# Splitting half of the convolution mixers' weight blocks on GpSimd instead of VectorE

## The chip, the cores and the metric
The kernel runs on one core of one Trainium2 chip. The metric is device time in microseconds (us) of one launch; the median of three runs before the change is 2242.76 us (2242.38 to 2246.66).

The core's engines are named as the profile names them: PE (TensorE matmuls), PEld (TensorE weight loads, which overlap PE), DVE (VectorE), ACT (ScalarE), POOL (GpSimd) and SP (SyncE, which here only issues DMAs). Each engine takes its own instructions strictly in order and waits at an instruction until what it needs has been signalled by the others.

## The reference
One inference step of a four-layer decoder trunk (1024 channels) for 256 prompt tokens and 8 x 4 sample tokens, 288 columns in all. Every layer is a token mixer and a squared-ReLU MLP with residuals; layers 0 and 3 use retention, layer 1 Mamba-2 SSD, layer 2 gated DeltaNet.

```python
for i in range(DEPTH):                       # DEPTH = 4
    h = _rms(x, norm_mix[i])
    out = (_retention, _ssd, _gdn)[i % 3](h, ...)
    x = x + out
    x = x + jnp.square(jax.nn.relu(_rms(x, norm_mlp[i]) @ w_up)) @ w_down

def _ssd(h, ...):                            # _gdn has the same frame
    z, xbc, dt = split(h @ w_in)             # 1024 x 6176 weights
    xbc, new_buf = _causal_conv(xbc, conv_buf, conv_w)   # 4 taps
    xbc = silu(xbc + conv_b)
    y, s_new = _decay_scan(c_out, b_in, xs * dt, log_a, s0)
    return _rms(y * silu(z)) * norm_w @ w_out            # 2048 x 1024 weights
```

The two mixers with a causal convolution in front of their scan, SSD and gated DeltaNet, are the "convolution mixers" of this text. All inputs and outputs are fp32.

## The kernel before
Activations lie transposed: 128 channels on the partitions, 288 tokens along the free dimension. Every product with a weight matrix goes through one routine, `dense` (lines 188 to 232). To keep fp32 precision with the fast fp32r matmul, it splits each operand into a high and a low part and adds three products: high x high, low activations x high weights, high activations x low weights (lines 227, 228, 229).

The weights pass through three steps. SP loads a block `raw` of 1 MB (two buffers). The block is cut along its columns into tiles, and each tile along the contraction into two halves of 128 x 512 elements: the loop over `kh` at line 207, whose first half has `kh` = 0. For each half ACT writes the high part, `wh` (line 212, a cast to fp32r), and then DVE the low part, `wl` = raw - wh (line 215):

```python
self.last_cast = nc.scalar.copy(wh, src)
nc.vector.tensor_tensor(out=wl, in0=src, in1=wh, op=ALU.subtract)
```

`wh` and `wl` have four buffers each, so two tiles are held. A tile of two halves feeds 24 matmuls of 288 columns. Both splitting instructions are issued at high priority (`HP`), so the scheduler, which writes the fixed order of every engine's queue ahead of time from priorities and its own cost estimates, sets them early.

`units` (lines 510 to 535) runs a mixer in four units. Of unit m it weaves the chain of small steps that the scan needs (`step(m)`: the finish of unit m-1, then `chain(m)`) with dense work that fills PE meanwhile: the gate projection, the output projection of an earlier unit, and the input projection of unit m+1. At the entry, before any weaving, `proj(0)` runs alone; at the end `out(3)` runs alone. The names of the chain that come up below:

- entry of SSD and gated DeltaNet: `ms` (line 333, DVE) and `rs_y` (line 268, a power on POOL) make the norm's factor, which PE broadcasts; then the step sizes go through a softplus on DVE (lines 883 to 894) to `la` (line 996, SSD) or `g` (line 1315), on which the first cumulative sums on PE wait.
- convolution: `U` gets the past columns by a copy on POOL (line 808), `cacc` adds the taps on DVE (line 832), `tl` keeps the last columns (line 818 at first, on DVE).
- SSD unit: `xw`, `xws`, `bm`, `cm` are products on POOL (lines 1062, 1078, 1114, 1112), `Et` the decay matrices (line 1167).
- gated DeltaNet unit (`prep`): `L` (line 1484, DVE, eight instructions), `Et` (line 1493, POOL), `kd` (line 1542, POOL), `Ls` (line 1498 on, DVE), `sm` (lines 1535 to 1537, DVE), `lm` (line 1565, POOL), `T` (line 1568, DVE) and then `ps_Y` on PE.

`gates_tok` calls `dense` with weights that are already loaded (`pre`), for the 32 columns of the step sizes.

Of the kernel before, what the change touches and what calls it, by code (L numbers as in the profile page):

```python
# [12 lines left out]
ALU = mybir.AluOpType  # L13
# [110 lines left out]
def run(gen):  # L124
    for _ in gen:
        pass


class K:
    def __init__(self, ctx, tc, I, O, C, layers):  # L130
        self.tc, self.nc, self.I, self.O, self.C = tc, tc.nc, I, O, C
        self.layers = layers
        self.hold, self.started = [], False
        self.ahead = 0
        nc = self.nc
        E = ctx.enter_context
        self.const = E(tc.tile_pool(name="const", bufs=1))
        self.xp = E(tc.tile_pool(name="xp", bufs=1))
        self.raw = E(tc.tile_pool(name="raw", bufs=2))
        self.wsp = E(tc.tile_pool(name="wsp", bufs=4))  # L140
        self.actp = E(tc.tile_pool(name="actp", bufs=1))
        self.tmp = E(tc.tile_pool(name="tmp", bufs=3))
        self.psd = E(tc.tile_pool(name="psd", bufs=3, space=PSUM))
        self.psm = E(tc.tile_pool(name="psm", bufs=5, space=PSUM))

        def cload(name, shape=None, src=None):
            a = I[name] if src is None else src
            t = self.const.tile(list(a.shape) if shape is None else shape, F32, name="c_" + name)
            nc.sync.dma_start(t, a)
            return t  # L150

        self.ones = self.const.tile([128, 128], F32, name="ones")
        nc.vector.memset(self.ones, 1.0)
        self.mhalf = self.const.tile([128, 1], F32, name="mhalf")
        nc.vector.memset(self.mhalf, -0.5)
        self.vec = self.const.tile([128, 128], F32, name="vec")
        with tc.high_priority(1000):
            self.ident = cload("ident")
# [29 lines left out]
    def dense(self, xh, xl, w, evac, pre=None):  # L188
        nc, tc = self.nc, self.tc
        n, kt = w.shape[1], len(xh)  # L190
        cw = 2048 // kt
        sw = 1024 // kt
        for c0 in range(0, n, cw):
            cn = min(cw, n - c0)
            if pre is None:
                raw = self.raw.tile([128, kt, cn], F32, name="raw", tag="raw")
                with self.tc.high_priority(HP):
                    step = cn if self.started or c0 else sw
                    for s0 in range(0, cn, step):
                        self.last_load = nc.sync.dma_start(raw[:, :, s0:s0 + step],  # L200
                                          w[:, c0 + s0:c0 + s0 + step].rearrange("(k p) n -> p k n", p=128))
            else:
                raw = pre
            for s0 in range(0, cn, sw):
                sn = min(sw, cn - s0)
                hs, ls = [], []
                for kh in range(0, kt, kt // 2):
                    wh = self.wsp.tile([128, kt // 2, sn], F32R, name="wh", tag="wh")
                    wl = self.wsp.tile([128, kt // 2, sn], F32R, name="wl", tag="wl")
                    src = raw[:, kh:kh + kt // 2, s0:s0 + sn]  # L210
                    with self.tc.high_priority(HP):
                        self.last_cast = nc.scalar.copy(wh, src)  # L212
                        first = self.hold.pop(0) if self.hold else None
                        with tc.issue_after(first.ins) if first else nullcontext():
                            nc.vector.tensor_tensor(out=wl, in0=src, in1=wh, op=ALU.subtract)  # L215
                    hs += [wh[:, k] for k in range(kt // 2)]
                    ls += [wl[:, k] for k in range(kt // 2)]
                for o in range(0, sn, 128):
                    os = slice(o, min(o + 128, sn))
                    self.ahead -= 1  # L220
                    if 0 <= self.ahead < 2:
                        ps = self.ps("psd", "s")[:, 0:T]
                    else:
                        ps = self.psd.tile([128, T], F32, name="psd", tag="d")
                    po = ps[:os.stop - o]
                    for k in range(kt):
                        nc.tensor.matmul(po, lhsT=hs[k][:, os], rhs=xh[k], start=(k == 0), stop=False)  # L227
                        nc.tensor.matmul(po, lhsT=hs[k][:, os], rhs=xl[k], start=False, stop=False)  # L228
                        self.last_mm = nc.tensor.matmul(po, lhsT=ls[k][:, os], rhs=xh[k], start=False,  # L229
                                                        stop=(k == kt - 1))  # L230
                    evac((c0 + s0 + o) // 128, ps)
                    yield kt * 3 * 0.124
# [274 lines left out]

        yield from self.dense(act[0], act[1], w[m * 512:(m + 1) * 512, :], ev)

    def units(self, proj, chain, gate, fin, w, i, side=None):  # L510
        acts = {}

        def finish(m):
            acts[m] = self.act_quarter(m)
            yield from fin(m, *acts[m])

        def out(n):
            yield from self.w_out(w, n, acts.pop(n), i)

        def step(m):  # L520
            if m:
                yield from finish(m - 1)
            yield from chain(m)

        self.ahead = 5
        run(proj(0))
        for m in range(4):
            fill = [gate(m)]
            fill += [out(0)] if m == 1 else [out(1)] if m == 3 else []
            rest = [proj(m + 1)] if m < 3 else []  # L530
            if side:
                rest = [self.both(side(m), rest[0])] if rest else [side(m)]
            self.weave(step(m), *fill, *rest)
        self.weave(finish(3), out(2))
        run(out(3))


# [400 lines left out]
    def ssd(self, ctx, j, i):  # L938
        nc, tc, I, O, C = self.nc, self.tc, self.I, self.O, self.C
# [3 lines left out]
        w = I["ssd_w_in"][j]  # L943
# [92 lines left out]
        units = {}  # L1036
# [203 lines left out]
                                           op0=ALU.mult, op1=ALU.mult)  # L1240
                    self.split(o, ah[a], al[a])

        self.units(proj, scan, gate, fin, I["ssd_w_out"][j], i)

# [2 lines left out]
    def gdn(self, ctx, j, i):  # L1249
        nc, tc, I, O, C = self.nc, self.tc, self.I, self.O, self.C  # L1250
# [3 lines left out]
        w = I["gdn_w_in"][j]  # L1254
# [101 lines left out]
        units = {}  # L1356
# [400 lines left out]
            yield from prep(m)  # L1757
            yield from loop(m)

        self.units(proj, scan, gate, fin, I["gdn_w_out"][j], i, sample)  # L1760
        self.later = lambda pool: self.gdn_states(pool, j)

    def gdn_states(self, pool, j):
# [83 lines left out]
```

## Time and profile before
| | |
|---|---|
| median of 3 runs | 2242.76 us |
| profiled execution, its own time | 2250.74 us |
| its span, first to last instruction | 2248.6 us |
| mean granted TensorE clock | 0.98 of full speed |
| PE, PEld busy | 97 %, 89 % of the span |
| DVE, ACT, POOL busy | 69 %, 55 %, 26 % |
| SSD mixer | about 536 to 890 us of the span |
| gated DeltaNet mixer | about 1088 to 1480 us |

The profiled execution is one run of its own, 8.0 us above the median of the others. A matmul's busy time is longer than its share of PE's pace, because matmuls are pipelined: each of 288 columns is shown as 0.29 us, but the next starts 0.13 us later. So PE's idle time, the granted clock and what PE waited for say more than its busy share. In the two convolution mixers DVE and POOL work on the chains beside the weights; in the MLPs they do little else than the weights, the evictions and the residual.

### The profile page before, as it was taken

How to read it: one execution, taken by the hardware profiler on the slowest of the kernel's cores; microseconds unless marked ns; L12 is line 12 of the kernel's file. 1: busy time of each engine (PE TensorE's matmuls, PEld its weight loads, DVE VectorE, ACT ScalarE, POOL GpSimd, SP SyncE). 2: the span in 40 equal slices, each digit the busy share in tenths (PEclk: the TensorE clock that was granted, in tenths of full speed). 3: DMA queues.
4: the chain of work that ended last, by engine and by line, in shares of the span. 5: the costliest groups of instructions: out<-in, count | busy, mean ns of one | idle time of the engine just before them, and what ended most of it. 6: DMA issues, size and time to landing. Idle time of an engine off the chain costs nothing. (4 is left out here: it accounts for less than half of the span.)

```text
span 2248.6 us, 43174 instructions
## 1 busy us (share of the span) xinstructions
PE 2172.1 (97%) x16348; PEld 1996.7 (89%) x16348; DVE 1555.2 (69%) x3195; ACT 1242.9 (55%) x2823; POOL 586.0 (26%) x622
## 2 busy tenths in 40 slices
PE   9999999999999999999899999999999999999998
PEld 7878899998889889999888888889899779889998
DVE  6777775557898887555786786577766677776554
ACT  4444455545687766554466676476644444445454
POOL 2100113333322322333332232134333001103333
PEclk9999999999899999999989999899999999999999
DMA  7776765545446544554443442277765666764553
GB/s 208 255 254 206 248 195 160 169 151 161 128 145 192 171 143 139 172 169 151 148 127 106 121 140 93 90 207 236 226 187 188 228 230 218 237 222 158 163 167 115
DMA packets 404219, 394.96 MB, mean 176 GB/s; under 512 B 13003, under 2 KB 353716, under 8 KB 403916
## 3 DMA queue, kind: packets, MB, share of 16 engines
q1 hardware_dynamic: 403852, 391.96, 55.0%
q8 instruction: 128, 2.10, 0.4%
q14 instruction: 79, 0.65, 0.1%
q10 hardware_dynamic: 96, 0.20, 0.0%
q0 software_dynamic: 64, 0.07, 0.0%
HBM read 333.49 MB, written 58.69 MB: 174 GB/s over the span
## 5 line engine op out<-in xcount | busy, mean ns | idle before, releaser
L212 ACT CAST wh<-raw 128x512 fp32r<-128x512 f32 x1024 | 627.8, 620 | 675.4 <-PE psd L228 629.7
L215 DVE TENSOR_TENSOR wl<-raw,wh 128x512 fp32r<-128x512 f32 x1024 | 743.3, 733 | 309.0 <-ACT wh L212 290.5
L227 PE MATMUL psd<-xh,wh 128*128 128x288 f32 x2576 | 776.4, 302 | 6.5 <-ACT xh L302 4.6
L228 PE MATMUL psd<-xl,wh 128*128 128x288 f32 x2576 | 773.4, 300 | 4.4 <-DVE xl L303 3.2
L229 PE MATMUL psd<-xh,wl 128*128 128x288 f32 x2576 | 770.3, 299 | 3.8 <-DVE wl L215 3.8
L227 PEld LDWEIGHTS psd<-xh,wh 128*128 128x128 f32 x2576 | 487.7, 190 | 27.5 <-issue 11.1
L228 PEld LDWEIGHTS psd<-xl,wh 128*128 128x128 f32 x2576 | 491.6, 191 | 18.2 <-issue 7.5
L229 PEld LDWEIGHTS psd<-xh,wl 128*128 128x128 f32 x2576 | 490.7, 191 | 11.6 <-DVE wl L215 6.7
L227 PE MATMUL psd<-ah,wh 128*128 128x288 f32 x1536 | 463.4, 302 | 5.0 <-DVE x L447 2.8
L229 PE MATMUL psd<-ah,wl 128*128 128x288 f32 x1536 | 459.8, 299 | 6.8 <-DVE wl L215 6.7
L228 PE MATMUL psd<-al,wh 128*128 128x288 f32 x1536 | 460.8, 300 | 1.6 <-issue 1.1
L227 PEld LDWEIGHTS psd<-ah,wh 128*128 128x128 f32 x1536 | 292.6, 191 | 15.3 <-ACT wh L212 5.3
L229 PEld LDWEIGHTS psd<-ah,wl 128*128 128x128 f32 x1536 | 293.9, 191 | 10.2 <-DVE wl L215 9.1
L228 PEld LDWEIGHTS psd<-al,wh 128*128 128x128 f32 x1536 | 293.3, 191 | 10.0 <-issue 7.8
L487 POOL TENSOR_TENSOR x<-x,dn 128x288 f32<-128x288 f32 x120 | 148.7, 1239 | 239.4 <-DVE dn L485 239.4
L468 POOL TENSOR_TENSOR a<-v 128x288 f32<-128x288 f32 x128 | 109.6, 857 | 270.7 <-ACT v L467 269.7
L731 DVE SCALAR_TENSOR_TENSOR S<-S,ps_up 128x512 f32<-128x512 f32 x128 | 83.4, 685 | 53.5 <-PE ps_up L730 50.8
L832 DVE SCALAR_TENSOR_TENSOR cacc<-U,cw,cacc 128x312 f32<-128x312 f32 x192 | 105.3, 554 | 13.8 <-ACT cacc L827 11.8
L470 DVE TENSOR_TENSOR al<-a,ah 128x288 fp32r<-128x288 f32 x128 | 59.9, 468 | 68.7 <-POOL a L468 67.9
L268 POOL TENSOR_TENSOR rs_y<-ms,mhalf 128x3 f32<-128x3 f32 (+3 forms) x37 | 36.2, 981 | 231.2 <-DVE ms L747 170.7
L808 POOL COPY U<-cb 128x24 f32<-128x24 f32 x64 | 34.4, 543 | 208.0 <-DVE cacc L832 140.4
L485 DVE TENSOR_TENSOR dn<-psd,rb 128x288 f32<-128x288 f32 x128 | 58.2, 455 | 40.4 <-PE psd L229 40.4
(512 smaller groups left out, 2618.5 us busy)
## 6 DMA issues: line engine op xcount, KB each, us to landing
raw<-mlp_w_up SPq DMA_DIRECT2D x64, 1024.0 KB
raw<-mlp_w_down SPq DMA_DIRECT2D x64, 1024.0 KB
raw<-ret_w_in SPq DMA_DIRECT2D x32, 1024.0 KB
S<-state_ret SPq DMA_DIRECT2D x64, 512.0 KB
s_ret<-S SPq DMA_DIRECT2D x64, 512.0 KB
raw<-ssd_w_in SPq DMA_DIRECT2D x24, 1024.0 KB
raw<-gdn_w_in SPq DMA_DIRECT2D x24, 1024.0 KB
raw<-ret_w_in SPq DMA_DIRECT2D x32, 512.0 KB
```

What stands on the lines that cost most here:

```text
L212: self.last_cast = nc.scalar.copy(wh, src)
L215: nc.vector.tensor_tensor(out=wl, in0=src, in1=wh, op=ALU.subtract)
L227: nc.tensor.matmul(po, lhsT=hs[k][:, os], rhs=xh[k], start=(k == 0), stop=False)
L228: nc.tensor.matmul(po, lhsT=hs[k][:, os], rhs=xl[k], start=False, stop=False)
L229: self.last_mm = nc.tensor.matmul(po, lhsT=ls[k][:, os], rhs=xh[k], start=False, stop=(k == kt - 1))
L268: self.nc.gpsimd.tensor_tensor(out=y[rows], in0=ms[rows], in1=self.mhalf[rows].broadcast_to([rows.stop - rows.start, n]), op=ALU.pow)
L468: nc.gpsimd.tensor_tensor(out=a, in0=v, in1=v, op=ALU.mult)
L470: nc.vector.tensor_tensor(out=al[o], in0=a, in1=ah[o], op=ALU.subtract)
L485: nc.vector.tensor_tensor(out=t, in0=ps, in1=rb2, op=ALU.mult)
L487: e.tensor_tensor(out=self.x[o], in0=self.x[o], in1=t, op=ALU.add)
L731: nc.vector.scalar_tensor_tensor(out=S[:, b, z], in0=S[:, b, z], scalar=C["g4"][h], in1=up, op0=ALU.mult, op1=ALU.add)
L832: nc.vector.scalar_tensor_tensor(out=acc[:, 0:n], in0=u, scalar=wk, in1=acc[:, 0:n], op0=ALU.mult, op1=ALU.add)
```

## The change
`dense` picks the engine of the low part: while `share` is set, the second half of every tile (`kh` not 0, and not the preloaded gate weights) is subtracted by GpSimd; the first half, and everything outside, stays on VectorE. `units` sets `share` for its whole run except `out(3)`; only `ssd` and `gdn` ask for it.

```diff
+        self.share = False
...
-                            nc.vector.tensor_tensor(out=wl, in0=src, in1=wh, op=ALU.subtract)
+                            e = nc.gpsimd if self.share and kh and pre is None else nc.vector
+                            e.tensor_tensor(out=wl, in0=src, in1=wh, op=ALU.subtract)
...
-    def units(self, proj, chain, gate, fin, w, i, side=None):
+    def units(self, proj, chain, gate, fin, w, i, side=None, share=False):
...
         self.ahead = 5
+        self.share = share
         run(proj(0))
...
         self.weave(finish(3), out(2))
+        self.share = False
         run(out(3))
...
-        self.units(proj, scan, gate, fin, I["ssd_w_out"][j], i)
+        self.units(proj, scan, gate, fin, I["ssd_w_out"][j], i, share=True)
...
-        self.units(proj, scan, gate, fin, I["gdn_w_out"][j], i, sample)
+        self.units(proj, scan, gate, fin, I["gdn_w_out"][j], i, sample, share=True)
```

In the queues, 120 of the 1044 `wl` instructions go from DVE to POOL, 60 in each mixer; the orders of the other engines change a little inside these two mixers, and nowhere else. Lines of the changed kernel are 2 to 4 higher.

POOL's queue in the `prep` of the last gated DeltaNet unit, before (`rs_y` and `eq` end the norms of queries and keys; `T` and `Sd` come after `lm`):

```order
L268 TENSOR_TENSOR rs_y<-ssq,mhalf 128x10
L1444 TENSOR_SCALAR eq<-ssq 128x4
L1445 TENSOR_SCALAR eq<-ssq 128x1
L1493 TENSOR_TENSOR Et<-Et,gm 128x256 x4
L1542 TENSOR_TENSOR kd<-ktok,ge 128x512 x2
L1565 TENSOR_TENSOR lm<-sm,c_gdn_lms 128x128
L1582 TENSOR_TENSOR at_18436<-sm,c_gdn_b_11523 128x128
L1565 TENSOR_TENSOR lm<-sm,c_gdn_lms 128x128
L1533 COPY T_13996<-Tm 32x8x32 x2
```

and the same place in the changed kernel:

```order
L217 TENSOR_TENSOR wl<-raw,wh 128x512 x2
L270 TENSOR_TENSOR rs_y<-ssq,mhalf 128x10
L1448 TENSOR_SCALAR eq<-ssq 128x4
L1449 TENSOR_SCALAR eq<-ssq 128x1
L1497 TENSOR_TENSOR Et<-Et,gm 128x256 x3
L217 TENSOR_TENSOR wl<-raw,wh 128x512
L1497 TENSOR_TENSOR Et<-Et,gm 128x256
L1546 TENSOR_TENSOR kd<-ktok,ge 128x512 x2
L217 TENSOR_TENSOR wl<-raw,wh 128x512
L1569 TENSOR_TENSOR lm<-sm,c_gdn_lms 128x128
L1586 TENSOR_TENSOR at_18436<-sm,c_gdn_b_11523 128x128
L1569 TENSOR_TENSOR lm<-sm,c_gdn_lms 128x128
```

Two `wl` now stand ahead of `rs_y`, one between the third and fourth `Et` and one between `kd` and `lm`.

DVE's queue at that place, from the `L` on, before:

```order
L1484 SCALAR_TENSOR_TENSOR L<-Et,be_18148,gm 128x128 x8
L215 TENSOR_TENSOR wl<-raw,wh 128x512 x3
L1498 STREAM_TRANSPOSE Ls<-Lc 128x512
L1535 TENSOR_TENSOR sm<-ps_gram_18102,c_gdn_m_11529 128x32
L1499 TENSOR_SCALAR Ls<-Ls,c_gdn_h_11533 128x256
L1536 SCALAR_TENSOR_TENSOR sm<-ps_gram_18102,sc_18154,c_gdn_m_11529 128x32
L1500 SCALAR_TENSOR_TENSOR Ls<-Ls,c_gdn_h_11533 128x256
L1537 TENSOR_TENSOR sm<-sm,e_17945 128x64
```

and in the changed kernel:

```order
L1488 SCALAR_TENSOR_TENSOR L<-Et,be_18148,gm 128x128 x8
L217 TENSOR_TENSOR wl<-raw,wh 128x512
L552 SCALAR_TENSOR_TENSOR sg<-th,psd 128x288
L1539 TENSOR_TENSOR sm<-ps_gram_18102,c_gdn_m_11529 128x32
L1540 SCALAR_TENSOR_TENSOR sm<-ps_gram_18102,sc_18154,c_gdn_m_11529 128x32
L1502 STREAM_TRANSPOSE Ls<-Lc 128x512
L217 TENSOR_TENSOR wl<-raw,wh 128x512
L1503 TENSOR_SCALAR Ls<-Ls,c_gdn_h_11533 128x256
L1541 TENSOR_TENSOR sm<-sm,e_17945 128x64
L1504 SCALAR_TENSOR_TENSOR Ls<-Ls,c_gdn_h_11533 128x256
```

Behind the eight `L` there stood three `wl`, now one, and `sm` moves up before `Ls`.

DVE's queue at the entry of SSD, before (`ms` starts the norm's factor):

```order
L303 SCALAR_TENSOR_TENSOR xl_6500<-x_93,vec,xh_6499 128x288
L215 TENSOR_TENSOR wl<-raw,wh 128x512 x4
L333 TENSOR_SCALAR ms<-ps_st 128x3
L215 TENSOR_TENSOR wl<-raw,wh 128x512
L910 TENSOR_TENSOR gr<-psd,rb 32x288
```

and in the changed kernel, where POOL has two `wl` in front of `rs_y`:

```order
L305 SCALAR_TENSOR_TENSOR xl_6500<-x_93,vec,xh_6499 128x288
L217 TENSOR_TENSOR wl<-raw,wh 128x512 x2
L335 TENSOR_SCALAR ms<-ps_st 128x3
L914 TENSOR_TENSOR gr<-psd,rb 32x288
L281 TENSOR_TENSOR xr<-x_86,rb 128x288
```

`ms` comes two `wl` sooner, and `gr`, which follows the broadcast factor, three.

## Rows read from the trace of the kernel before

**Rows 1.** The page, part 1: busy us, share of the span, instructions.

```profile
PE 2172.1 (97%) x16348; PEld 1996.7 (89%) x16348; DVE 1555.2 (69%) x3195; ACT 1242.9 (55%) x2823; POOL 586.0 (26%) x622
```

**Rows 2.** Stretches: length, busy PE, PEld, DVE, ACT, POOL (x), clock, DMA, GB/s.

```profile
536.00:580.00 44.00, 36.69 (x219) 32.65 (x219) 35.49 (x97) 22.96 (x55) 12.21 (x15) 0.81 0.47 134
580.00:890.00 310.00, 301.27 (x2337) 272.63 (x2337) 261.07 (x550) 219.64 (x605) 83.06 (x80) 1.00 0.52 156
890.00:1088.00 198.00, 198.00 (x1494) 197.45 (x1493) 110.61 (x185) 101.06 (x197) 67.05 (x64) 0.99 0.53 167
1088.00:1135.00 47.00, 39.46 (x249) 35.33 (x248) 39.96 (x118) 26.36 (x64) 16.81 (x25) 0.89 0.42 130
1135.00:1480.00 345.00, 325.96 (x3221) 290.67 (x3220) 247.48 (x658) 219.60 (x590) 89.11 (x123) 0.96 0.39 119
```

**Rows 3.** What PE waited for, 536 to 900 us: total, times, longest.

```profile
PE ps_cs L850 <- DVE tl L818: 2.7, 1, 2.7
...
PE ps_ct L1003 <- DVE la L996: 1.8, 1, 1.8
...
PE ps_bc L342 <- POOL rs_y L268: 1.4, 2, 0.9
```

**Rows 4.** The same, 1088 to 1480 us.

```profile
PE psd L229 <- DVE wl L215: 7.4, 6, 2.6
PE ps_Y L1569 <- DVE T L1568: 4.1, 3, 2.9
PE ps_dif L1302 <- DVE tl L818: 3.5, 1, 3.5
```

**Rows 5.** Tile wl, 540 to 890 us: duration ns min/median/max, first and last start.

```profile
L215 DVE TENSOR_TENSOR wl<-raw,wh x135: 670/685/2177, 542.1 to 889.0; 128x512 fp32r<-128x512 f32 x135
```

**Rows 6.** Group of wl, 520 to 920 us: busy us, mean ns, idle before.

```profile
L215 DVE TENSOR_TENSOR wl<-raw,wh 128x512 fp32r<-128x512 f32 x162 | 118.8, 745 | 24.9 <-ACT wh L212 18.3 <-PE psd L229 3.8 <-PE psd L227 0.9
```

**Rows 7.** POOL's groups over the span, products of 512 and 1024 columns.

```profile
L1114 POOL TENSOR_TENSOR bm<-bst,c_maskb 128x1024 fp32r<-128x1024 f32 x8 | 15.7, 1962 | 13.4 <-PE ps_sT L1125 7.0 <-DVE bst L1095 3.9 <-PE ps_up L1003 2.5
...
L1542 POOL TENSOR_TENSOR kd<-ktok,ge 128x512 f32<-128x512 f32 x8 | 10.4, 1316 | 0.3
...
L1712 POOL TENSOR_TENSOR Sd<-S,ge 128x512 f32<-128x512 f32 x4 | 4.2, 1040 | 42.4 <-issue 33.5 <-ACT S L1710 8.9
```

**Rows 8.** Timeline of DVE, 607 to 612 us: start, length, instruction.

```profile
608.57 1.12 DVE L1146 SCALAR_TENSOR_TENSOR S<-S,dec,ps_up 128x128 f32<-128x128 f32 x4 [0.36 <-PE ps_up L1003]
609.61 2.12 DVE L215 TENSOR_TENSOR wl<-raw,wh 128x512 fp32r<-128x512 f32 x2
```

**Rows 9.** Timeline of POOL, the same stretch.

```profile
608.67 1.90 POOL L1114 TENSOR_TENSOR bm<-bst,c_maskb 128x1024 fp32r<-128x1024 f32 x1 [2.46 <-PE ps_up L1003]
```

**Rows 10.** Timeline of DVE in the last prep, 1396 to 1412 us.

```profile
1399.67 3.63 DVE L1484 SCALAR_TENSOR_TENSOR L<-Et,be,gm 128x128 f32<-128x128 f32 x8
1403.22 3.26 DVE L215 TENSOR_TENSOR wl<-raw,wh 128x512 fp32r<-128x512 f32 x3
```

**Rows 11.** Timeline of POOL, the same stretch.

```profile
1400.35 0.77 POOL L1493 TENSOR_TENSOR Et<-Et,gm 128x256 f32<-128x256 f32 x1 [0.72 <-DVE L L1484]
...
1408.30 0.46 POOL L1565 TENSOR_TENSOR lm<-sm,c_gdn_lms 128x128 f32<-128x128 f32 x1 [0.92 <-DVE Ls L1506]
...
1409.13 0.47 POOL L1565 TENSOR_TENSOR lm<-sm,c_gdn_lms 128x128 f32<-128x128 f32 x1
```

**Rows 12.** Timeline of PE, the same stretch.

```profile
1399.41 0.30 PE L227 MATMUL psd<-ah,wh 128*128 128x288 f32 x1
1399.54 0.29 PE L228 MATMUL psd<-al,wh 128*128 128x288 f32 x1
...
1403.96 0.61 PE L229 MATMUL psd<-ah,wl 128*128 128x288 f32 x1 [2.64 <-DVE wl L215]
1404.36 0.44 PE L227 MATMUL psd<-ah,wh 128*128 128x288 f32 x1
1404.60 0.44 PE L228 MATMUL psd<-al,wh 128*128 128x288 f32 x1
```

## Prediction
> **What bounds the kernel now.** I read the page's busy shares first, then the busy times by stretch, then what PE waited for in the two mixers that change, then the groups and the timeline around the weights' low parts. The page has PE busy 97 % of the span, DVE 69 % and POOL 26 % [rows 1]: it looks like a kernel bound by PE with two helpers that have room. By stretch it is less even [rows 2]. In the MLP between the two mixers PE is never idle (198.00 of 198.00 us) at a clock of 0.99, so nothing can be won there, and nothing is changed there. In the four stretches of the two mixers, 746 us together, PE is idle for 7.3 + 8.7 + 7.5 + 19.0 = 42.6 us. Their granted clocks of 0.81, 1.00, 0.89 and 0.96 cost 44 x 0.19 + 47 x 0.11 + 345 x 0.04 = 27.4 us more. These 70 us are all that any change of the helpers can win, and 0.64 us of clock goes with each us of idle time. DVE is busy 584 of the 746 us (78 %), POOL 201 us (27 %).
>
> Of the waits of PE that the trace names, two kinds stand behind DVE. The matmul that needs the low part waits for `wl` itself, 7.4 us in six waits, all in gated DeltaNet [rows 4]. And chain steps wait for work that stands in DVE's queue between `wl` instructions: `tl` 2.7 and `la` 1.8 in SSD [rows 3], `T` 4.1 and `tl` 3.5 in gated DeltaNet [rows 4], together 12.1 us. For POOL, PE waits 1.4 us at `rs_y` in SSD [rows 3].
>
> [...]
>
> **The change part by part.** *Off DVE.* 120 `wl` leave its queue. One takes 0.685 us where nothing disturbs it [rows 5], so 82 us leave, of 584.
>
> *Onto POOL.* No POOL instruction of before subtracts two full operands of 128 x 512. The nearest rows are `Sd`, 1.04 us with the same size and one broadcast operand, with nothing on DVE in its way, `kd`, 1.32 us, the same among `wl`, and `bm`, twice the size, 1.96 us [rows 7]. The first is the lower bound, the last an upper one; I take 1.2, near the two of the same size. That is 144 us more on POOL (125 to 235), which brings it from 27 to 46 % of the 746 us. It has the room.
>
> *What it takes back from DVE.* POOL and DVE do not run side by side here. While POOL makes `bm` from 608.67 to 610.57 [rows 9], the four `S` steps on DVE, which read PSUM, go on; the two `wl` that start at 609.61 take 2.12 us instead of 1.37, and end 1.16 us after `bm` does [rows 8]. So an instruction of DVE that reads two operands from SBUF stands still until POOL's is done. Two bounds for this. From today's mean: `wl` takes 0.745 us on average [rows 6] against 0.685 undisturbed, 8.8 % more, with POOL busy 27 %; with 19 points more that stretch grows by 6.2 %, 36 us of 584, and 46 us of the 82 remain as relief, 8 % of DVE's work. From the other side: if DVE, busy 78 % of the time, stood still in all of POOL's new 144 us, it would lose 112 us and be 30 us worse off. I take the first, since it is what the same queues show now, and keep the second as a rival.
>
> [...]
>
> *The waits for `wl`.* Half of the low parts no longer stand behind DVE's chain work, so I take half of the 7.4 us: -3.7. Bounds: 0 and -7.4.
>
> *The chain steps behind DVE.* DVE's idle share of 22 % grows by 8 points, about a third; of the 12.1 us I take a quarter, -3.0. Bounds: 0 (the strings of DVE are not shorter, only filled with standing still) and -12.1. At SSD's entry `ms` comes two `wl` sooner, 1.4 us by two of 0.685, but `rs_y` on POOL now stands behind two `wl` of its own, 2.4 us in an otherwise idle stretch; I take the two as even, and what is late next there is `la`.
>
> *The clock.* With 0.64 us for each of these 6.7 us: -4.3. Bounds: 0 and 19.5 x 0.64 = -12.5.
>
> *What POOL delays.* Whatever the chain has on POOL (`rs_y`, the decay and key products, `lm`) now queues behind `wl`, and `wl` behind the chain. In each of eight units I count two steps of POOL that PE's next chain step has to have and that no dense work covers, each behind half a `wl` (0.6 us) in 46 % of cases: 8 x 2 x 0.6 x 0.46 = +4.4. Bounds: 0 (dense matmuls cover it, as they nearly do today with 1.4 us) and a whole `wl` each time, 8 x 2 x 1.2 = +19.
>
> Nothing is taken from SP, and ACT makes as many casts as before. The three queues' other steps move by a few places in the two mixers; I price that at nothing, because the dense matmuls that fill PE are the same, and leave it in the range.
>
> Sum: -3.7 - 3.0 - 4.3 + 4.4 = -6.6 us on the profiled execution's 2250.74, 2244.1. That execution lies 8.0 us above the median of the runs, 2242.76, so I forecast 2236 us.
>
> **The rivals.** *The lock eats it.* DVE stands still in most of POOL's new time, its relief is nil or below, PE's 19.5 us of waits behind DVE stay, and POOL's lateness is paid: 0 to +4.4 us, about 2245, which is no change that can be measured. For it: most of DVE's time in these stretches is spent on instructions like `wl`, with two operands in SBUF. Against it: today's stretch of 8.8 % is far less than POOL's busy share, so DVE often has other things to do while POOL works. [...]
>
> *POOL starves PE in the `prep` (slower).* In a `prep` POOL's queue is `Et` four times, `kd` twice and `lm`, which waits for `sm` on DVE: from 1400.35 to 1409.60, 9.25 us [rows 11]. In the first of the four units no `wl` stands among these; in the one shown in the order two do. The four buffers hold two tiles, 48 matmuls at 0.13 us, 6.2 us of work. If the next `wl` (1.2 us) comes only after `lm`, PE stands for 9.25 + 1.2 - 6.2 = 4.2 us; in three of four units, with the clock, 3 x 4.2 x 1.64 = +20.7, less today's 7.4 x 1.64 = 12.1 that it replaces, plus the 4.4 of POOL's other delays: +13, or 2256 us. It decides from the point at which two `wl` of POOL lie more than 6.2 us apart while PE has only dense work left. For it: POOL waits in order, and `sm` comes late. Against it: the `wl` in the two gaps, and `sm` moving ahead of `Ls`.
>
> *Much more is won.* The waits behind DVE go almost whole, with their clock: two thirds of the 19.5 us and their clock, 13 + 8.3 = 21 us, 2221 with POOL's delays at nothing. For it: the clock's 27.4 us hang on a few gaps that DVE makes. Against it: the lock.
>
> **How the numbers follow.** The forecast's kind of outcome, a small gain, gets 0.40 and its own range of 2226 to 2243; much more won 0.10; the lock 0.25; POOL starving PE 0.25. A measurement of this kernel tells about 0.2 %, 4.5 us, from no change: 2238.3 to 2247.2 counts as the same. Faster: 0.32 of the small gain, 0.10 of the large one and 0.02 of the lock's, 0.44. Same: 0.08, 0.19 of the lock's and 0.03 of the starving, 0.30. Slower: 0.04 of the lock's and 0.22, 0.26. The range reaches from the large gain, 2221, to just past the starving, 2258.
>
> **What would show it.** Right: in the changed profile DVE's busy time in the four stretches falls by some 46 us and POOL's rises by some 144; the waits for DVE's `wl` halve, and the clocks of 0.81, 0.89 and 0.96 rise. The lock's case: DVE falls by less than 20 us, `wl` on DVE has a mean well above 0.8 us, and the stretches keep their length. Starving: the low-part matmul waits for POOL's `wl`, 3 us and more at a time, near `lm`, with the lower clock behind it. The forecast is wrong if a POOL `wl` takes nearer 2 us than 1.2, since then 46 % becomes 58 % and all of DVE's relief is gone, or if PE's new waits are at steps that no row of before names.

## The result and the profile after

The changed kernel takes 2311.12 us (median of 4 runs, 2298.79 to 2313.27) against 2244.71 for the kernel before in the same series: a ratio of 1.0292, 95 % interval 1.0270 to 1.0313. It is slower by 66 us, where 2236 was forecast and 2258 was the end of the range. The profiled execution took 2298.79 us, 48 more than that of before, so its trace shows some three quarters of the loss.

Page of the changed kernel, part 1, as in [rows 1]:

```profile
PE 2181.4 (95%) x16348; PEld 2003.9 (87%) x16348; DVE 1562.0 (68%) x3075; ACT 1241.5 (54%) x2823; POOL 729.9 (32%) x742
```

DVE has 120 instructions fewer and is busy 7 us longer. The same by stretch, with the bounds laid at the same steps of the work as in [rows 2] (length, then busy PE, PEld, DVE, ACT, POOL, then the clock):

```profile
533.00:582.00 49.00, 39.07 (x224) 33.86 (x222) 37.95 (x93) 23.67 (x58) 18.67 (x22) 0.83 0.42 121
582.00:906.00 324.00, 306.37 (x2336) 276.10 (x2335) 253.45 (x493) 221.08 (x604) 150.21 (x133) 0.99 0.50 150
906.00:1103.00 197.00, 196.08 (x1490) 195.30 (x1489) 110.12 (x185) 99.74 (x194) 66.78 (x64) 1.00 0.52 166
1103.00:1156.00 53.00, 42.37 (x254) 37.61 (x253) 41.16 (x112) 27.13 (x66) 25.65 (x32) 0.84 0.38 116
1156.00:1528.00 372.00, 330.24 (x3215) 294.85 (x3213) 260.92 (x605) 218.65 (x594) 150.26 (x176) 0.94 0.36 111
```

The MLP in the middle kept its length (197 against 198 us). The four stretches of the mixers grew from 746 to 798 us. PE's idle time in them rose from 42.6 to 9.9 + 17.6 + 10.6 + 41.8 = 79.9 us, +37, and what the clock costs (49 x 0.17 + 324 x 0.01 + 53 x 0.16 + 372 x 0.06 = 42.4 us against 27.4) by +15: together the 52 us. DVE is busy 593.5 us there, against 584.0: with the forecast's 82 us counted as gone, 92 came back. POOL rose by 143.6 us, from 201.2 to 344.8.

The low part in the whole span, by engine (busy us, mean ns | idle before it), and VectorE's convolution step `cacc`:

```profile
L217 DVE TENSOR_TENSOR wl<-raw,wh 128x512 fp32r<-128x512 f32 x904 | 666.0, 743 | 301.7 <-ACT wh L213 291.1 <-PE psd L230 3.3 <-PE psd L231 2.4
L217 POOL TENSOR_TENSOR wl<-raw,wh 128x512 fp32r<-128x512 f32 x120 | 166.1, 1384 | 168.9 <-ACT wh L213 128.5 <-PE ps_kS L1306 11.5 <-issue 9.1
L836 DVE SCALAR_TENSOR_TENSOR cacc<-U,cw,cacc 128x312 f32<-128x312 f32 x192 | 127.7, 669 | 18.2 <-ACT cacc L831 12.8 <-ACT cacc L833 2.6 <-POOL wl L217 0.7
```

`cacc` before the change:

```profile
L832 DVE SCALAR_TENSOR_TENSOR cacc<-U,cw,cacc 128x312 f32<-128x312 f32 x192 | 105.3, 554 | 13.8 <-ACT cacc L827 11.8 <-ACT cacc L829 0.8
```

What PE waited for, 533 to 906 us, as in [rows 3]:

```profile
PE ps_bc L344 <- POOL rs_y L270: 6.0, 3, 3.3
PE ps_ct L1007 <- DVE la L1000: 3.6, 1, 3.6
PE ps_xt L1063 <- DVE xs L838: 2.3, 1, 2.3
...
PE ps_cs L854 <- DVE tl L822: 1.2, 1, 1.2
```

and 1103 to 1528 us, as in [rows 4]:

```profile
PE ps_Y L1573 <- DVE T L1572: 7.0, 3, 4.4
PE psd L231 <- DVE wl L217: 7.0, 6, 3.0
PE ps_wq L1306 <- ACT wy L1591: 4.9, 2, 2.8
PE ps_W L1306 <- DVE Ls L1518: 4.2, 3, 2.1
PE ps_o L1306 <- ACT lkv L1623: 4.0, 1, 4.0
PE ps_gc L1306 <- DVE g L1319: 3.4, 1, 3.4
...
PE ps_dif L1306 <- DVE tl L822: 2.1, 1, 2.1
...
PE psd L231 <- POOL wl L217: 1.6, 1, 1.6
```

The waits for low parts are about what they were (7.0 + 1.6 us against 7.4). What is new are the chain's small steps, on all three helpers: `Ls`, `g`, `wy`, `lkv`, `xs` stand in no row of before.

PE's longest single wait, in the third `prep`; [rows 10 to 12] show the fourth of before. First DVE (start, length, instruction):

```profile
1369.91 1.17 DVE L217 TENSOR_TENSOR wl<-raw,wh 128x512 fp32r<-128x512 f32 x1
1371.00 1.05 DVE L1541 TENSOR_TENSOR sm<-sm,e 128x64 f32<-128x64 f32 x1
...
1373.42 0.53 DVE L1572 TENSOR_TENSOR T<-c_ident,lm 128x128 f32<-128x128 f32 x1 [0.40 <-POOL lm L1569]
```

POOL at the same time:

```profile
1370.61 2.37 POOL L1546 TENSOR_TENSOR kd<-ktok,ge 128x512 f32<-128x512 f32 x2
1372.94 0.45 POOL L1569 TENSOR_TENSOR lm<-sm,c_gdn_lms 128x128 f32<-128x128 f32 x1
```

and PE:

```profile
1369.35 0.29 PE L231 MATMUL psd<-xh,wl 128*128 128x288 f32 x1
1374.01 0.47 PE L1573 MATMUL ps_Y<-c_ident,T 128*128 128x128 f32 x1 [4.37 <-DVE T L1572]
...
1374.52 0.44 PE L230 MATMUL psd<-xl,wh 128*128 128x288 f32 x1
1374.76 0.44 PE L231 MATMUL psd<-xh,wl 128*128 128x288 f32 x1
```

The product `sm` of 128x64, both operands in SBUF, takes 1.05 us while POOL makes `kd` (0.21 in the first `prep` of before, where POOL did nothing beside it). `lm` needs `sm`, stands behind `kd` on POOL, and `T` needs `lm`. PE's dense work ran out at 1369.6, it stood 4.37 us, and afterwards the dense matmuls start 0.24 us apart instead of 0.13: the granted clock is 0.50 from 1374 to 1376 us and was 1.00 from 1360 to 1369. Behind the 2.64 us of [rows 12] it was 0.50 as well (1404 to 1406.5 us). The stop at `sm` comes from `kd`, which was POOL's work before the change too; a new `wl` of POOL (1364.90 to 1366.34) had stopped the first `L` of this `prep`, which took 1.37 us where eight took 3.63 before. PE waits as long for `T` in kernels without these stops (below), so this place shows how a stop passes down the chain and does not measure what the stops cost.

### The profile page after: what moved, and what is told of

Same layout as the page of the kernel before. It is cut to its first block, busy times and chain, and to the rows that moved or that the text cites. A ratio compares the mean times of both kernels' runs of the same rounds, so it can differ in the third digit from the quotient of the medians.

```text
span 2297.0 us, 43235 instructions
## 1 busy us (share of the span) xinstructions
PE 2181.4 (95%) x16348; PEld 2003.9 (87%) x16348; DVE 1562.0 (68%) x3075; ACT 1241.5 (54%) x2823; POOL 729.9 (32%) x742
## 5 line engine op out<-in xcount | busy, mean ns | idle before, releaser
L217 DVE TENSOR_TENSOR wl<-raw,wh 128x512 fp32r<-128x512 f32 x904 | 666.0, 743 | 301.7 <-ACT wh L213 291.1
L217 POOL TENSOR_TENSOR wl<-raw,wh 128x512 fp32r<-128x512 f32 x120 | 166.1, 1384 | 168.9 <-ACT wh L213 128.5
L836 DVE SCALAR_TENSOR_TENSOR cacc<-U,cw,cacc 128x312 f32<-128x312 f32 x192 | 127.7, 669 | 18.2 <-ACT cacc L831 12.8
L323 POOL TENSOR_TENSOR acc<-acc,sq 128x288 f32<-128x288 f32 x54 | 46.9, 868 | 131.3 <-ACT sq L322 130.5
```

Of the source, the lines that this page charges most:

```text
L217: e.tensor_tensor(out=wl, in0=src, in1=wh, op=ALU.subtract)
L323: nc.gpsimd.tensor_tensor(out=acc, in0=acc, in1=sq, op=ALU.add)
L836: nc.vector.scalar_tensor_tensor(out=acc[:, 0:n], in0=u, scalar=wk, in1=acc[:, 0:n], op0=ALU.mult, op1=ALU.add)
```

## The experiments

All times are medians, "+" is against the kernel before in the same series, and the ratio stands with its 95 % interval. Edits are shown shortened. Three theories were put to them: the **lock** (the name the prediction's first rival has for it: VectorE stands still while GpSimd works on two SBUF operands), GpSimd's **queue** (the chain's steps there come late), and the changed **order** of the work.

**Which instructions stand still.** A kernel of its own with the four strings beside five kinds of GpSimd work:

```
for beside in (nothing, two, fill, copy, power):
    5 x V.tensor_tensor(out=o, in0=a, in1=b)          # SBUF, SBUF, 128x512
    5 x V.tensor_scalar(out=o, in0=a, scalar1=2.0)    # SBUF, 128x512
    5 x V.tensor_tensor(out=o, in0=ps, in1=b)         # PSUM, SBUF, 128x512
    5 x V.tensor_tensor(out=o[:, 0:64], ...)          # SBUF, SBUF, 128x64
```

> A kernel of its own, which computes nothing of the reference: VectorE runs five subtracts of two SBUF operands of 128x512, five multiplies of one SBUF operand by a constant, five subtracts with one operand in PSUM, and five subtracts of two SBUF operands of 128x64; the whole string first alone and then beside GpSimd doing, one after another, two-operand subtracts of 128x512, fills, copies and powers of 128x10. Theory of the lock (VectorE stands still while GpSimd works on SBUF): the 128x512 subtract takes 0.6 to 0.7 us alone and 1.3 us or more beside GpSimd's subtract, the 128x64 one 0.2 us alone and up to 1.5 us there, the PSUM form is the same in every part; the multiply by a constant stands still as well, as one of 1.30 us instead of 0.20 did in the changed kernel. Theories of GpSimd's queue and of the changed order: VectorE's times are the same in every part within 10 %.

Timeline of DVE, in the order alone, beside subtracts, beside fills, beside copies, beside powers:

```profile
7.23 3.59 DVE L58 TENSOR_TENSOR o<-a,b 128x512 f32<-128x512 f32 x5
10.86 2.27 DVE L60 TENSOR_SCALAR o<-a 128x512 f32<-128x512 f32 x5
...
16.79 1.26 DVE L64 TENSOR_TENSOR o<-a,b 128x64 f32<-128x64 f32 x5
...
18.27 7.36 DVE L58 TENSOR_TENSOR o<-a,b 128x512 f32<-128x512 f32 x5
25.67 6.97 DVE L60 TENSOR_SCALAR o<-a 128x512 f32<-128x512 f32 x5
32.67 3.59 DVE L62 TENSOR_TENSOR o<-ps,b 128x512 f32<-128x512 f32 x5
36.30 3.43 DVE L64 TENSOR_TENSOR o<-a,b 128x64 f32<-128x64 f32 x5
...
40.03 3.60 DVE L58 TENSOR_TENSOR o<-a,b 128x512 f32<-128x512 f32 x5
43.66 3.66 DVE L60 TENSOR_SCALAR o<-a 128x512 f32<-128x512 f32 x5
...
58.48 4.75 DVE L58 TENSOR_TENSOR o<-a,b 128x512 f32<-128x512 f32 x5
...
73.47 3.60 DVE L58 TENSOR_TENSOR o<-a,b 128x512 f32<-128x512 f32 x5
```

Beside GpSimd's subtract the 128x512 string takes 7.36 us instead of 3.59, the 128x64 one 3.43 instead of 1.26, the one-operand one 6.97 instead of 2.27; the one that reads PSUM stays at 3.59. A fill stops the one-operand form (3.66 us instead of 2.27) and not the subtract (3.60), a copy costs the subtract a third (4.75), and the powers, 2.09 us each in the mean, leave it at 3.60. One by one, a stopped 128x512 subtract takes 1.63 us instead of 0.69 beside GpSimd subtracts of 1.59: 0.94 us more, which I read as what is left of GpSimd's instruction. The lock is there, and GpSimd's fill is a way to load its queue almost without it.

**The load without the relief.** VectorE keeps all its low parts, GpSimd repeats the second half's into a tile that nobody reads:

```
  nc.vector.tensor_tensor(out=wl, in0=src, in1=wh, op=ALU.subtract)
+ if share: nc.gpsimd.tensor_tensor(out=dum, in0=src[480 of 512], in1=wh[480 of 512], op=ALU.subtract)
```

> Every low part stays on VectorE as before the change, and beside it GpSimd makes the second half's subtract once more (480 of its 512 columns) into a tile that nobody reads. The order of PE's and VectorE's work is nearly that of before. Theory of the lock: VectorE loses some 90 us to GpSimd's 150 and is relieved of nothing, so it is slower than the changed kernel or as slow, +60 to +150 us, 2305 to 2395. Theory of GpSimd's queue (rs_y and the chain's other steps there come late behind the subtracts): +20 to +35 us, 2265 to 2280, with VectorE's times unchanged. Theory of the changed order: nothing, 2240 to 2250.

2327.49 us, +83, 1.0366 (1.0332 to 1.0400), in the range of the lock's theory. No matmul and no step of the chain reads this work (only SP's loads wait for it, 22.0 us in all, since it reads `raw`), and the order is nearly that of before; GpSimd's longer queue is in the +83 as well. VectorE's busy time, 1555.2 us before, by the page's part 1:

```profile
PE 2185.3 (94%) x16348; PEld 2006.1 (87%) x16348; DVE 1646.6 (71%) x3195; ACT 1242.4 (54%) x2823; POOL 759.6 (33%) x742
```

+91.4 us for the same 3195 instructions. The changed kernel, whose VectorE does 82 us less work, is only 17 us faster than this one (+66 against +83).

**The relief without the lock.** The second half's low part is a fill, once or three times over:

```
- e.tensor_tensor(out=wl, in0=src, in1=wh, op=ALU.subtract)
+ if share: nc.gpsimd.memset(wl, 0.0)      # once, or three times
```

> As the changed kernel, but the second half's low part is a fill with zeros on GpSimd (0.53 us by the row of before, instead of 1.38 us), so its part of the product is left out. VectorE is relieved of the same 120 subtracts, and the order of the work is close to that of the changed kernel. Theory of the lock, or of the queue: the loss goes with GpSimd's added time, 63 us instead of 166: +25 us, 2270; if a fill leaves VectorE alone, the lock's theory expects a gain instead, 2221 to 2240, and the queue's +25. Theory of the changed order: the loss stays, +50 to +70 us, 2295 to 2315.

> As the kernel with one fill, but GpSimd fills the second half's low part with zeros three times over (its part of the product is left out), so that it is busy longer than with the subtract: 3 x 0.55 = 1.65 us instead of 1.38, 198 us instead of 166. In the study of VectorE's forms a fill left subtracts of two SBUF operands as fast as alone (3.60 against 3.59 us for five) and held up only the one-operand form. Theory of GpSimd's queue: the chain's steps wait behind the fills as behind the subtracts, +50 to +75 us, 2295 to 2320. Theory of the lock: without the standing still of VectorE's two-operand work most of the loss is gone, 0 to +20 us, 2245 to 2265.

One fill: 2248.65 us, +4.6, 1.0010 (0.9995 to 1.0025), in none of the ranges. Three: 2253.62 us, +9.9, 1.0033 (1.0017 to 1.0049), with GpSimd busy longer than in the changed kernel (740.7 us). The order of the work is close to the changed kernel's in both, so the order makes little of the 66 us, and most of the loss is gone with the lock. The gain that the lock's theory allowed, 2221 to 2240, did not come.

A fill does not wait for ScalarE's cast, as the subtract does for 128.5 us in all. So a third form waits first:

```
+ if share: nc.gpsimd.tensor_copy(wl[:, 0, 0:1], wh[:, 0, 0:1]); 2 x nc.gpsimd.memset(wl, 0.0)
```

> The kernels with fills have a gap: a fill does not wait for ScalarE's high part, so GpSimd's queue does not stand at it as at the subtract (128.5 us of waiting for that cast in the changed kernel). Here GpSimd first copies one column of the high part, and so waits for the cast, and then fills twice (the second half's low part is left out): the queue is held as in the changed kernel, some 1.25 us and the wait for each, almost without the lock. If the queue's waiting was what the kernels with fills lacked, +40 to +66 us, 2285 to 2311. If the lock makes the loss, as with three fills, +5 to +20 us, 2250 to 2265.

2255.15 us, +13.2, 1.0059 (1.0039 to 1.0078). Page, part 1, VectorE's low parts and the convolution step:

```profile
PE 2177.2 (97%) x16348; PEld 2000.5 (89%) x16348; DVE 1496.1 (66%) x3075; ACT 1242.9 (55%) x2823; POOL 715.8 (32%) x982
...
L217 DVE TENSOR_TENSOR wl<-raw,wh 128x512 fp32r<-128x512 f32 x904 | 663.1, 739 | 300.5 <-ACT wh L213 291.7 <-PE psd L231 3.2 <-PE ps_up L1813 0.9
...
L836 DVE SCALAR_TENSOR_TENSOR cacc<-U,cw,cacc 128x312 f32<-128x312 f32 x192 | 107.3, 561 | 31.2 <-ACT cacc L831 22.9 <-ACT cacc L833 6.0 <-POOL U L812 0.4
```

GpSimd is as busy as in the changed kernel (716 against 730 us) and its queue stands at the same casts (161.4 us of waiting for them, 128.5 there), but VectorE is busy 66 us less, and `cacc` is back at 561 ns from 669. Of these 66 us `wl` itself bears 3 (663.1 us here, 666.0 in the changed kernel) and `cacc` 20: it is mostly the chain's instructions that stand still. Putting the subtract in the place of copy and fills costs 66.4 - 13.2 = 53 us (some 7 either way by the two intervals): that is the lock, as far as fills are free of it.

**The relief alone.** The low part that the change moves is made by nobody:

```
- e.tensor_tensor(out=wl, in0=src, in1=wh, op=ALU.subtract)
+ if share: wl = wh
```

> The upper bound of any relief: where the changed kernel gives the low part to GpSimd, here nobody makes it (the matmul takes the high part in its place, so its part of the product is wrong by that). VectorE is rid of all 120 subtracts, 82 us, and GpSimd gets nothing. If relief of VectorE has the worth that the prediction gave it (6.7 us of waits and their clock for 46 us, up to 21 us for all of it), 2224 to 2238. If it has none (VectorE has slack at 69 %, and only standing still in the chain counts), or if the order of the work, which changes as much as in the changed kernel, takes it back, 2240 to 2252.

2239.41 us, -5.4, 0.9970 (0.9956 to 0.9984), between the two ranges, at the edge of no worth. VectorE's busy time is 1491.2 us, 64 less than before:

```profile
PE 2169.1 (97%) x16348; PEld 1995.3 (89%) x16348; DVE 1491.2 (66%) x3075; ACT 1241.7 (55%) x2823; POOL 558.1 (25%) x622
```

All that taking these 120 subtracts away from VectorE can win, with the order that comes with it, is 5 us. And since only 64 us leave when nobody makes them, GpSimd's subtracts gave 1562.0 - 1491.2 = 71 us back to VectorE in the changed kernel, not 92.

The lock also shows in what PE waits for, in us over the whole span. The kernels with GpSimd's subtract are, in this order, the changed one, the one with the load but no relief, and the one with the subtract in two halves (below); those without it have one fill, three fills, copy and two fills, nobody:

| step | before | with GpSimd's subtract | without it |
|---|---|---|---|
| `Ls` (DVE) | none | 4.2, 9.8, 4.4 | 0.6, 0.7, 1.1, 1.2 |
| `g` (DVE) | 0.3 | 3.4, 3.5, 2.3 | 0.5, 0.9, 0.3, 0.2 |
| `la` (DVE) | 1.8 | 3.6, 3.9, 2.9 | none, 1.0, none, none |
| `rs_y` (POOL) | 6.5 | 13.0, 10.3, 10.7 | 7.1, 6.6, 7.2, 7.7 |
| `T` (DVE) | 4.1 | 7.0, 5.2, 8.7 | 8.8, 7.4, 5.0, 6.2 |

`Ls`, `g`, `la` and `rs_y` come late with GpSimd's subtract and only with it. `T`, which had the longest single wait, is waited for as long without it: that comes with the moved work and its order.

**Dose and place.** Every second tile only; the change in one mixer alone; the subtract in two halves; the share in the MLPs instead of the mixers:

```
e = nc.gpsimd if self.share and kh and self.turn() and pre is None else nc.vector    # every second
self.units(..., share=True)                                                          # in one of the two
for a in (0, kt // 4): nc.gpsimd.tensor_tensor(out=wl[:, a:a + kt // 4], ...)        # two halves
self.share = i in (1, 2)                                                             # in mlp, not in units
```

> As the changed kernel, but only every second tile is shared, so GpSimd makes 60 low parts instead of 120. Theories of the lock and of the queue: half of the loss, +33 us, 2270 to 2285. Theory of the changed order: the order differs from before as much as with 120, so the loss is about the same, +50 to +70 us.

> The change in the SSD mixer alone. In the changed kernel's profile the SSD mixer took 20 of the 54 us that the two mixers lost. If each mixer pays for its own standing still (lock), +22 to +28 us, 2266 to 2273. If the loss comes from what one mixer hands to the next (rival), the two kernels with one mixer each do not add up to +66 us.

> The change in the gated DeltaNet mixer alone, which took 34 of the 54 us in the changed kernel's profile. Lock: +38 to +46 us, 2282 to 2290, and with the SSD mixer's alone some +66. Rival: the sum is off by more than 15 us.

> As the changed kernel, but GpSimd makes each of its low parts in two subtracts of half the columns, so that VectorE gets its turn after some 0.7 us instead of 1.38; GpSimd's total is the same or a little more. If the lateness of single steps makes the loss (VectorE's step waits for at most one GpSimd instruction), a good part of it goes: +25 to +45 us, 2270 to 2290. If the total of the time in which VectorE stands still makes it (91 us), nothing changes: +60 to +75 us, 2304 to 2319.

> The mixers are as before, and the share is made in the MLPs of the two layers that have them, where GpSimd makes the second half of 128 low parts (120 in the changed kernel) and PE has dense work alone. If the loss needs a chain of small steps that PE waits for, then the same standing still of VectorE costs next to nothing here: -2 to +8 us, 2242 to 2252. If it goes by VectorE's lost time wherever that is, +40 to +66 us.

Half the dose: 2275.64 us, +31.6, 1.0139 (1.0115 to 1.0162), half the loss. SSD alone: 2263.37, +19.7, 1.0095 (1.0060 to 1.0130); gated DeltaNet alone: 2298.60, +54.9, 1.0232 (1.0204 to 1.0261); both miss their ranges (+22 to +28 and +38 to +46), one below, one above; their sum is 75 us against 66, which the intervals allow, so that each mixer pays for itself stands. Two halves: 2305.59, +60.7, 1.0255 (1.0227 to 1.0283). GpSimd's pieces are 0.83 us instead of 1.38, their total 194 us instead of 166; shorter stops, as long in sum, cost about the same. That the length of the single stop makes the loss fell with it.

The MLPs: 2280.22, +35, 1.0135 (1.0096 to 1.0174), neither of the two answers. By the trace, taken on the slowest of its four executions (2287.78), the MLP after SSD, pure dense work, took 184.5 us instead of 183.2 with 55 of its 64 shared subtracts in that stretch. But VectorE hardly stood still there: its busy time fell from 102.6 to 73.6 us, by 29 of the 38 us of subtracts that left it, so some 9 us came back, 0.2 us for each subtract against 0.6 in the mixers. That dense work bears the same standing still, as the expectation had it, is therefore not shown; it bore a small one. Most of the loss lies elsewhere. The MLP after gated DeltaNet, beside which the states of that mixer are worked off, took 224.0 us instead of 210.9. Gated DeltaNet took 441 instead of 423: the last 55 us of it, in which ten of the next MLP's subtracts already run on GpSimd, are 8 us longer, with a wait of PE for `rs_y` of 6.6 us instead of 3.0; the other 10 us lie where GpSimd has no shared subtract, and where they come from stays open; the granted clock over the whole mixer was 0.92 against 0.95.

**The other way round.** If GpSimd's work stops VectorE, less of it should help the kernel before. From that kernel, with every low part on VectorE, `bm`, `kd` and `Sd` were given to ScalarE, then to VectorE; then most of the other two-operand work too; then only `Et`, with and without `qd`:

```
- G.tensor_tensor(out=bm, in0=bcm(bst[...], DB), in1=bc3(self.maskb, 128), op=ALU.mult)
+ for q in range(DB): A.activation(bm[:, q], bst[...], AF.Copy, scale=self.maskb[:, q:q + 1])   # ScalarE
+ V.tensor_tensor(out=bm, ...)                                                                  # VectorE
```

> Another way to use the lock, from the kernel before, with every low part on VectorE: three kinds of GpSimd's two-operand work (bm, kd, Sd: 30 us of its 201 us in the two mixers) go to ScalarE, as 112 scaled copies of 128x128 of about 0.39 us, 44 us. Lock: the changed kernel lost 62 us more than the one with a fill for 166 us of such work on GpSimd, 0.37 us for each, so 30 us less gives 11 us, less what ScalarE's longer queue takes back: 2228 to 2244. Rival (the standing still that before has is harmless, since VectorE is busy 69 %): no gain, and ScalarE's queue costs, 2244 to 2260.

> The kernel before, with bm, kd and Sd on VectorE instead of GpSimd. If a two-operand instruction on GpSimd keeps VectorE standing about as long as VectorE would take to do it (1.38 against 0.685 us for 512 columns), nothing is lost or a little won by taking it over: 2236 to 2246. If VectorE's queue is the worse place (it then stands in the way of the chain's steps whether they use the lock or not), slower by 5 to 15 us.

> As the last, and xw, xws, cm, Et, qd and the gate's product go to VectorE as well: most of GpSimd's two-operand work in the two mixers, some 87 us, which VectorE does in about half. If GpSimd's lock is what costs in the kernel before, faster, 2225 to 2240; if VectorE's queue is the worse place, slower by 10 to 30 us.

> As the kernel with bm, kd and Sd on VectorE, with Et and qd on VectorE too and the rest left on GpSimd. In the kernel with all of it the gated DeltaNet mixer was 6 us shorter and the SSD mixer 1 us longer than before; if that holds here, 2232 to 2239. If it was scatter, 2240 to 2247.

> As the last, with qd left on GpSimd: if two-operand work on GpSimd costs as the lock's theory has it, between the kernel without Et (2240) and the last one, 2234 to 2241; if VectorE's queue is the worse place for Et, 2242 to 2250.

ScalarE: 2249.72, +6.0, 1.0028 (1.0012 to 1.0044), where the rival had it and not the lock. VectorE: 2239.67, -5.2, 0.9975 (0.9958 to 0.9993). With most of the rest: 2244.75, -0.1, 0.9999 (0.9980 to 1.0018), a miss for both answers. `Et` and `qd` besides: 2239.76, -5.0, 0.9975 (0.9962 to 0.9988), just past its range for a gain; `Et` only: 2239.29, -5.5, 0.9971 (0.9956 to 0.9987). Three of the five versions that take work *off* GpSimd beat the kernel before, by a quarter of a percent, with intervals that leave out 1. In the first VectorE is busy 1562.1 us, 7 more than before, though `bm`, `kd` and `Sd` take it 18.5 us there (9.7, 6.0 and 2.8), so some 12 us of standing still are gone. That the lock is the cause of those 5 us is likely and not shown: moving more gave nothing more, and the steps' places in the queues moved too.

## Why the prediction was wrong

**What bounds the kernel** was read rightly: the loss lies in the four stretches, in idle time and clock, and not in the MLP.

**Off DVE, onto POOL.** 120 subtracts left, 82 us at their undisturbed length, as worked out, though VectorE's busy time falls by only 64 where nobody makes them. One took 1.38 us on POOL in the mean, not the 1.2 chosen from [rows 7], and 166 us in all, inside the bounds of 125 to 235.

**What it takes back from DVE** is the step that failed, twice over. First its size: "46 us of the 82 remain as relief" came from stretching the 8.8 % of [rows 5, 6] by POOL's busy share, to 36 us that come back. Measured, 71 came back (92 if all 82 are counted as gone), twice as much, and short of the other bound, 112, which I kept as a rival; no relief was left. The mean hid a mixture. Some of what POOL did before stops little (in the study five subtracts took 3.60 us beside powers and beside fills, 3.59 alone), and a two-operand subtract stops every form tried that reads SBUF alone (7.36 us instead of 3.59, 6.97 instead of 2.27, 3.43 instead of 1.26); a busy share of one kind is no price for the other. My sentence that an instruction "that reads two operands from SBUF stands still until POOL's is done" holds for POOL's subtract and was too narrow, as the one-operand multiply did too (6.97 us instead of 2.27), and too wide, as POOL's powers, 2.09 us each, left five of the two-operand subtracts at 3.60 us against 3.59.

Second, and worth more: the standing still was priced as busy time given or not given back. The rival that took the relief to be nil ended at 0 to +4.4 us, as if VectorE's busy sum set the time; a term for the standing still of chain steps is missing. The runs give two prices that are ten times apart. Taking 64 us of low parts off VectorE is worth 5.4 us, 0.08 for each. Putting 66 us of standing still on it costs 53 us, 0.81 for each. The reading that fits: the low parts are made ahead into four buffers, so PE seldom waits for them (16 waits for VectorE's over the span, 10.5 us before and 10.2 in the changed kernel), while the lock stops whatever VectorE is at on SBUF alone, and the chain's steps wait for one another, with nothing made ahead. So the sum of VectorE's time could stay the same while `cacc`, `sm`, `Ls`, `g` and `la` came late. That the prices differ is shown by the pair 0.08 and 0.81; that this is the reason is supported by where the 66 us fell (3 on `wl`, 20 on `cacc`) and by PE's new waits, and is argued beyond that. By the runs the loss is -5.4 of relief, 18.6 of GpSimd's queue and 53.2 of the lock, 66.4 in all; the forecast had -11.0, +4.4 and nothing.

**The waits for `wl`,** forecast -3.7 us: -0.4 on DVE and +1.6 on POOL. **The chain steps behind DVE,** forecast -3.0: `la`, `tl` and `T`, 12.1 us before, are 13.9, and new ones stand beside them. **The clock,** forecast -4.3: +15 beside 37 us more of idle time, 0.40 us for each; the granted clock rose from 0.81 to 0.83 in the first of the four stretches and fell in the others (1.00 to 0.99, 0.89 to 0.84, 0.96 to 0.94).

**What POOL delays,** forecast +4.4 with bounds of 0 and +19: between the kernel without the low part and the one that waits, copies and fills lie 13.2 + 5.4 = 18.6 us, which holds this and the little that the order changes. The upper bound was right and the value I took too small; of all terms beside the lock it is the largest.

**The rivals.** "The lock eats it" had the mechanism and VectorE's sum (relief below nil), and failed in its price. "POOL starves PE in the `prep`" named the place, but not the wait: PE waited for POOL's `wl` once, 1.6 us, and for the chain behind POOL and DVE the rest. "Much more is won" was out of reach, as nothing but 5 us was there to be won.

**The signs.** The last one for a wrong forecast came: PE's new waits are at `Ls`, `wy`, `lkv` and `xs`, which no row of before names. The lock's sign, a mean of `wl` on DVE well above 0.8 us, did not come (0.80 in the four stretches), because the stops fell on the chain's instructions. The other condition, that at 2 us for a POOL `wl` "all of DVE's relief is gone", was summed wrongly: by the forecast's own rule some 20 us would be left.

## What to carry to other kernels

Before work moves from VectorE to GpSimd, ask not how much VectorE is relieved, but which of its instructions stand in a chain and read SBUF only: here GpSimd's two-operand subtracts stopped them (by 0.94 us beside subtracts of 1.59 in the study, 71 us for 120 in the mixers), and the stop was paid on the chain (53 us for 66 us of standing still), while the relief was in work that is made ahead anyway (5.4 us for 64 us less of it). Price relief and delay apart: a kernel in which nobody does the moved work gives the most that the move can win, and one in which the other engine does it in vain gives its cost, and together they cost two runs. Where a chain is the limit, moving two-operand work the other way, from GpSimd to VectorE, may win a little even though VectorE is the busier of the two (69 against 26 % here); in these runs it was a quarter of a percent in three tries of four, with the cause not shown.

## What was unexpected of the hardware

GpSimd's powers over 128x10, 2.09 us each in the mean, left VectorE's subtracts at 3.60 us for five, as when alone, so the length of a GpSimd instruction in the profile does not tell how long it stops VectorE. A VectorE multiply of one SBUF operand by a constant is stopped beside GpSimd's subtract for as long as the two-operand subtract, 0.94 us each (1.37 us instead of 0.43, 1.63 instead of 0.69), and took 1.6 times its length beside a plain fill (3.66 us for five instead of 2.27). The relation shows the other way too: in the study GpSimd's subtract took 1.59 us beside VectorE's two-operand subtract and 1.26 beside the one that reads PSUM, its copy 0.95 and 0.61. In the mixers, with 120 subtracts more to do, GpSimd's other work got 22.5 us shorter (143.6 us more busy, of which 166.1 are the subtracts), and where nobody makes these low parts GpSimd is busy 558.1 us instead of 586.0 with the same instructions: I read this as GpSimd standing still for VectorE as well.
